# First matrix of each feed-forward as 2x2x2 block products: seven products in place of eight, sums of blocks formed on chip

## The chip, the cores and the metric

The kernel runs on one core of a Trainium2 chip. The metric is the device time of one launch in microseconds. Before the change it is 1934.65 us, the median of three runs (1934.33 to 1936.84).

The engines that matter: TensorE (PE in the profile; its weight loads are PEld) multiplies, VectorE (DVE) and ScalarE (ACT) work elementwise, SyncE (SP) only issues the transfers here, and GpSimd (POOL) sets a few tiles to zero.

## The reference

Two layers of three sublayers each: a feed-forward, a mixer (attention and a short convolution side by side) and a second feed-forward. The model width is 1024, there are 512 tokens, and a feed-forward has 2816 hidden columns, each with a gate and an up column. Everything is in single precision. The mixer's inside is not touched by the change.

```python
def _swiglu(h, w1, w2):
    g, up = jnp.split(h @ w1, 2, axis=-1)
    return (jax.nn.silu(g) * up) @ w2
...
def reference(x, c, w_ada, b_ada, norm_g, w_in, q_norm_g, k_norm_g, conv_w, conv_b,
              w_out, ffn_w1, ffn_w2):
    b = x.shape[0]
    for layer in range(DEPTH):
        mod = (jax.nn.silu(c) @ w_ada[layer] + b_ada[layer]).reshape(b, N_SUB, N_MOD, D_MODEL)
        shift = mod[:, :, 0, None, :]
        scale = mod[:, :, 1, None, :]
        gate = mod[:, :, 2, None, :]
        def ada(z, i):
            return _rmsnorm(z, norm_g[layer, i]) * (1.0 + scale[:, i]) + shift[:, i]
        x = x + 0.5 * gate[:, 0] * _swiglu(ada(x, 0), ffn_w1[layer, 0], ffn_w2[layer, 0])
        x = x + gate[:, 1] * _mixer(ada(x, 1), w_in[layer], q_norm_g[layer], k_norm_g[layer],
                                    conv_w[layer], conv_b[layer], w_out[layer])
        x = x + 0.5 * gate[:, 2] * _swiglu(ada(x, 2), ffn_w1[layer, 1], ffn_w2[layer, 1])
    return x
```

## The kernel before

All activations are kept transposed: channels on the partitions, the 512 tokens along the free axis, so x is eight tiles of 128x512. Every operand of the big products is held as two halves, a rounded one (hi) and the rest (lo), and a product of two operands is three matmuls: hi by hi, hi by lo, lo by hi (`product`, lines 173 to 177). The names in the trace are whi, wlo for weights, hh, hl for the normed input, hidh, hidl for the hidden tiles.

**Weights.** A unit is a block of 128x1024 (some 128x768) that is loaded into a raw tile by SP (four buffers); ScalarE copies it to whi (line 126) and VectorE subtracts to get wlo (line 127), with five buffers for each of the two. `weights` (line 143) hands out units in the fixed order of `_units` and lets `fetch` load and split two units ahead of the one in use.

**A feed-forward** (`ffn`, line 409) runs its 22 hidden tiles in three parts of 8, 8 and 6 (`PARTS`). For a hidden tile, a gate unit and an up unit are multiplied with the eight input tiles, each 8 x 3 matmuls of 512 columns into a PSUM bank (`gemm`); `finish` takes SiLU of the gate on ScalarE, multiplies by the up bank on VectorE (line 431) and splits the result (lines 319, 320). Behind a part, `Tail.run` (line 339) multiplies its hidden tiles with the second matrix, eight output tiles, and VectorE adds each into x (line 333). In the last part the last three output tiles are taken half by half of the tokens (256 columns), so that the next norm of the first half (sums of squares, `inv_rms`, `spread`, `modulate`) runs beside the products of the second half. `begin` (line 395) starts a feed-forward with four units of which first the one token half and then the other is multiplied, in the order in which `modulate` delivers tiles.

**Jobs.** The shift, scale and gate vectors of the next sublayers are dot products: a load of 512 KB and a VectorE operation of 128x1024 with a sum (`ada_job`, line 192). 16 of them stand in the start, the other 128 are queued by `later` and taken out by `next_job`: two behind each hidden tile, one behind each unit of the second matrix.

**Order.** The instructions are traced in program order; a list scheduler of the compiler then orders each engine's queue by that priority and by what is ready, and puts in the semaphores. Steps such as `inv_rms` are put among the products by counting product columns (`after`, `tick`).

## Time and profile before

| | before |
|---|---|
| median of three runs | 1934.65 us |
| span of the profiled execution | 1934.5 us |
| TensorE busy | 1909.2 us (99%), 9460 matmuls |
| VectorE busy | 1090.5 us (56%) |
| ScalarE busy | 675.0 us (35%) |
| moved by DMA | 253.95 MB, mean 131 GB/s |

The span reaches from the first to the last instruction of one execution. Busy time counts how long at least one instruction of the engine was running. Matmuls overlap, so the pitch between the starts of two of them says more than the duration of one. A line of the timeline gives the start, the duration, the engine, the line of the kernel, the operation and its tiles; "x3" is three instructions merged. In brackets stands the idle time before it and what ended it.

### The profile page before, as it was taken

The numbers are of one execution on the slowest core, as the hardware profiler recorded it, in microseconds if no ns is written. First come the engines' busy times: TensorE is split into PE (matmuls) and PEld (weight loads), VectorE is DVE, ScalarE is ACT, GpSimd is POOL, SyncE is SP. The second block draws the span as 40 slices with busy tenths as digits, with TensorE's granted clock in tenths as the row PEclk, the third lists the DMA queues.
The fourth block names the chain that finished last, engine by engine and source line by source line (L and its number), as shares of the span: only waits on it lengthen the run. The fifth ranks groups of instructions, "written<-read, shape, count | busy, mean of one in ns | idle before, by whom it ended". The sixth has DMA issues, their size and how long they took to land.

```text
span 1934.5 us, 24290 instructions
## 1 busy us (share of the span) xinstructions
PE 1909.2 (99%) x9460; PEld 1619.8 (84%) x9460; DVE 1090.5 (56%) x2074; ACT 675.0 (35%) x1110; POOL 12.2 (1%) x76
## 2 busy tenths in 40 slices
PE   6999999999999999999999999999999999999999
PEld 4888888899889888888898888888898898888888
DVE  8664564587866564433465545456977755333333
ACT  3322222355653322222332222223756533222121
POOL 0000000000000000000000000000000000000000
PEclk9999999999999999999999999999999999999999
DMA  8664564312223464222325646542222315222221
GB/s 340 207 218 156 170 218 131 109 55 68 97 66 121 147 219 157 99 98 90 122 98 190 211 149 197 184 130 77 78 76 88 109 66 177 96 98 98 98 82 60
DMA packets 73573, 253.95 MB, mean 131 GB/s; under 512 B 8049, under 2 KB 9073, under 8 KB 73458
## 3 DMA queue, kind: packets, MB, share of 16 engines
q1 hardware_dynamic: 73458, 252.40, 38.9%
q8 instruction: 74, 1.21, 0.3%
q14 instruction: 41, 0.34, 0.1%
HBM read 250.27 MB, written 2.10 MB: 130 GB/s over the span
## 4 chain that ended last, share of the span: by engine, by line
PE 98%; DVE 1%; DMA 0%; issue 0%; ACT 0%; SPq 0%; DVEq 0%
PE acc L175 31%; PE acc L177 30%; PE acc L176 30%; PE sb L530 1%; PE tp L521 1%; PE tp L550 1%; PE sb L175 1%; PE sb L176 1%; PE sb L177 1%; PE sb L560 1%; PE sb L561 1%; DVE ada L196 0%; DMA ada<-in_w_ada 0%; PE tp L290 0%; DVE ssq L282 0%; DVE wlo L127 0%
## 5 line engine op out<-in xcount | busy, mean ns | idle before, releaser
L126 ACT ACTIVATE whi<-raw 128x1024 fp32r<-128x1024 f32 (+1 forms) x344 | 350.0, 1021 | 986.7 <-PE acc L176 877.5
L175 PE MATMUL acc<-hh,whi 128*128 128x512 f32 (+1 forms) x1760 | 673.3, 384 | 0.0
L177 PE MATMUL acc<-hh,wlo 128*128 128x512 f32 (+1 forms) x1760 | 669.4, 381 | 0.0
L176 PE MATMUL acc<-hl,whi 128*128 128x512 f32 (+1 forms) x1760 | 665.5, 378 | 0.0
L127 DVE TENSOR_TENSOR wlo<-raw,whi 128x1024 fp32r<-128x1024 f32 (+1 forms) x344 | 402.8, 1174 | 245.9 <-ACT whi L126 217.5
L177 PEld LDWEIGHTS acc<-hh,wlo 128*128 128x128 f32 x1760 | 330.9, 188 | 66.1 <-DVE wlo L127 0.2
L176 PEld LDWEIGHTS acc<-hl,whi 128*128 128x128 f32 x1760 | 331.3, 188 | 62.3
L175 PEld LDWEIGHTS acc<-hh,whi 128*128 128x128 f32 x1760 | 331.1, 188 | 58.5 <-ACT whi L126 0.4
L175 PE MATMUL acc<-hidh,whi 128*128 128x512 f32 (+1 forms) x776 | 287.3, 370 | 0.0
L177 PE MATMUL acc<-hidh,wlo 128*128 128x512 f32 (+1 forms) x776 | 286.7, 369 | 0.0
L176 PE MATMUL acc<-hidl,whi 128*128 128x512 f32 (+1 forms) x776 | 286.6, 369 | 0.0
L333 DVE SCALAR_TENSOR_TENSOR x<-acc,fin,x 128x512 f32<-128x512 f32 (+1 forms) x130 | 87.9, 676 | 228.8 <-PE acc L177 228.3
L431 DVE TENSOR_TENSOR sg<-acc,sg 128x512 f32<-128x512 f32 x84 | 58.0, 691 | 252.4 <-PE acc L177 252.4
L196 DVE SCALAR_TENSOR_TENSOR ada<-ada,cb 128x1024 f32<-128x1024 f32 x144 | 172.2, 1221 | 17.5 <-DMA ada<-in_w_ada 11.2
L176 PEld LDWEIGHTS acc<-hidl,whi 128*128 128x128 f32 x776 | 146.3, 188 | 25.0
L177 PEld LDWEIGHTS acc<-hidh,wlo 128*128 128x128 f32 x776 | 146.2, 188 | 24.8
L175 PEld LDWEIGHTS acc<-hidh,whi 128*128 128x128 f32 x776 | 146.2, 188 | 24.8
L175 PE MATMUL acc<-whi,hh 128*128 128x384 f32 x256 | 89.5, 350 | 2.6 <-ACT hh L314 2.6
L176 PE MATMUL acc<-wlo,hh 128*128 128x384 f32 x256 | 86.6, 338 | 0.0
L177 PE MATMUL acc<-whi,hl 128*128 128x384 f32 x256 | 85.5, 339 | 0.0
L314 ACT ACTIVATE hh<-z,fin 128x256 fp32r<-128x256 f32 (+1 forms) x88 | 41.5, 522 | 58.0 <-DVE z L312 55.7
L320 DVE TENSOR_TENSOR hidl<-sg,hidh 128x512 fp32r<-128x512 f32 x88 | 60.0, 685 | 0.0
(89 smaller groups left out, 1308.3 us busy)
## 6 DMA issues: line engine op xcount, KB each, us to landing
raw<-in_w SPq DMA_DIRECT2D x176, 512.0 KB, 3.5
ada<-in_w_ada SPq DMA_DIRECT2D x128, 512.0 KB, 4.6
raw<-in_w2a SPq DMA_DIRECT2D x64, 512.0 KB, 3.5
raw<-in_w2b SPq DMA_DIRECT2D x32, 384.0 KB, 3.1
raw<-in_w_qkv SPq DMA_DIRECT2D x32, 384.0 KB, 3.1
raw<-in_w_gcu SPq DMA_DIRECT2D x24, 512.0 KB, 3.5
ada<-in_w_ada SPq DMA_DIRECT2D x8, 1024.0 KB, 8.4
raw<-in_w_out SPq DMA_DIRECT2D x16, 512.0 KB, 3.5
```

Of the source, the lines that this page charges most:

```text
L126: nc.scalar.activation(hi, raw, AF.Copy)
L127: nc.vector.tensor_tensor(out=lo, in0=raw, in1=hi.bitcast(F32), op=ALU.subtract)
L175: nc.tensor.matmul(out, a[0], b[0], start=first, stop=False)
L176: nc.tensor.matmul(out, a[0], b[1], start=False, stop=False)
L177: nc.tensor.matmul(out, a[1], b[0], start=False, stop=last)
L196: nc.vector.scalar_tensor_tensor(w, w, 1.0, cb, op0=ALU.mult, op1=ALU.mult, accum_out=raw[:, m, j:j + 1])
L314: nc.scalar.activation(hh[j][:, cols], z, AF.Identity, bias=shift)
L320: return nc.vector.tensor_tensor(out=lo, in0=v, in1=hi.bitcast(F32), op=ALU.subtract)
L333: nc.vector.scalar_tensor_tensor(x[j][:, cols], ps, gate, x[j][:, cols], op0=ALU.mult, op1=ALU.add)
L431: nc.vector.tensor_tensor(out=sg, in0=pu, in1=sg, op=ALU.mult)
L521: nc.tensor.transpose(pt[:, c * 128:(c + 1) * 128], p[:, c * 128:(c + 1) * 128], ident)
L530: nc.tensor.matmul(ps, v[c][:, i], z[:, c], start=c == m == 0, stop=c == n - 1 and m == 1)
```

## The change

The first matrix of a feed-forward is multiplied in blocks. The output of a pair of hidden tiles has two block rows (gate, up) and two block columns (first and second half of the tokens); the contraction has two blocks (the even and the odd tiles of the input). That would be eight block products. In Winograd's form of Strassen's algorithm there are seven:

| product | weights | tokens |
|---|---|---|
| 1 | gate, even | even, first half |
| 2 | gate, odd | odd, first half |
| 3 | gate odd - S | odd, second half |
| 4 | up, odd | V4 = odd first half - V6 |
| 5 | T = up even + up odd | V5 = even second half - even first half |
| 6 | S = T - gate even | V6 = odd second half - V5 |
| 7 | gate even - up even | V7 = odd second half - even second half |

One product is one unit of weights: two hidden tiles x four tiles of its contraction block x three, 24 matmuls of 256 columns. VectorE forms the four weight sums of each pair of hidden tiles in the raw tiles (`split_unit`), before the split in two halves, so a pair has seven units to split instead of four. Seven blocks are loaded for a pair instead of four (two gate blocks a second time). The four token sums are formed once for each norm, with the second token half (`Blocks.half`), and h becomes four tiles that hold seven operands each. Bank a of a pair takes products 1, 6, 7 and 4 one behind the other and is copied out by ScalarE in between (`done`), bank c takes 5 and 3, bank b takes 2; the other sums are VectorE's additions.

Around it: `_ffn_order` writes the order of units out by hand (products 1 and 2 of three pairs first, since they need the first token half alone; then the others of the first four pairs interleaved; from the fifth on pair by pair); the accumulation banks go from 4 and 2 to one group of 6; raw tiles go from 4 to 6 and now serve the jobs' loads too; weights are loaded two units further ahead than they are split; whi and wlo go from 5 to 4 and the separate buffers for the last units of the second matrix go; the last part begins with two output tiles side by side; the jobs of a third sublayer's gate move into the feed-forward before it; three jobs stand beside each of the first four pairs of the kernel, one beside each other pair, two behind each unit of the second matrix. In the mixer some small tiles move into the unused part of h.

```diff
-PARTS = ((0, 8), (8, 8), (16, 6))
-# The order of a mixer's products: q, k, v of pairs of heads, and the channel tiles of the convolution.
+NP = NF // 2
+PARTS = ((0, 4), (4, 4), (8, 3))
...
+LOADED = 2
...
+MOVING = {2: 0, 1: 1, 3: 2, 5: 3, 7: 4, 6: 5, 4: 6}
...
+def _ffn_order():
+    order = [[(0, 1), (0, 2)], [(1, 1), (1, 2)], [(2, 1)], [(2, 2)], [(0, 5), (0, 6)]]
+    order += [[u] for u in ((1, 5), (0, 7), (1, 6), (0, 4), (0, 3), (2, 5), (1, 7), (2, 6), (1, 4), (1, 3), (3, 1),
+                            (2, 7), (3, 5), (2, 4), (2, 3), (3, 6), (3, 2), (3, 7))]
+    ends = [p0 + n - 1 for p0, n in PARTS]
+    for n in range(3, NP):
+        if n > 3:
+            order += [[(n, 5)], [(n, 6)]]
+            if n - 1 in ends:
+                order += [[("part", ends.index(n - 1))]]
+            order += [[(n, 2)], [(n, 7)]]
+        if n + 1 < NP:
+            order += [[(n + 1, 1)]]
+        order += [[(n, 4)], [(n, 3)]]
+    return order + [[("part", len(PARTS) - 1)]]
...
-        return psum.tile([128, 512], F32, name="acc", tag="acc", bufs=4)
+        return psum.tile([128, 512], F32, name="acc", tag="acc", bufs=6)
...
+    s_bank = acc_bank
+    def half_kb(name):
+        return tmp.tile([128, S], F32, name=name, tag="ev", bufs=7)
...
+    def raw_tile(name="raw"):
+        return wp.tile([128, 1024], F32, name=name, tag="raw", bufs=6)
...
+        pool, bufs = place.get(key, (wp, 4))
...
+    def load_unit(key, src, n):
+        if key[0] != "w1":
+            return [load(src, n)]
+        b11, b12, b21, b22 = (src[b] for b in range(4))
+        return [load(b) for b in {1: (b11,), 2: (b12,), 3: (b12,), 4: (b22,), 5: (b21, b22), 6: (b11,), 7: ()}[key[4]]]
+    def split_unit(key, raws, n):
+        if key[0] == "w1":
+            pair, which = key[:4], key[4]
+            def combine(out, a, b, op):
+                nc.vector.tensor_tensor(out=out, in0=a, in1=b, op=op)
+            if which == 5:
+                a21, s = raws
+                combine(s, a21, s, ALU.add)
+                blocks[pair] = [a21, s]
+                raws = [s]
+            elif which == 6:
+                (a11,), (a21, s) = raws, blocks[pair]
+                combine(s, s, a11, ALU.subtract)
+                blocks[pair].append(a11)
+                raws = [s]
+            elif which == 7:
+                a21, _, a11 = blocks[pair]
+                combine(a11, a11, a21, ALU.subtract)
+                raws = [a11]
+            elif which == 3:
+                (a12,), s = raws, blocks.pop(pair)[1]
+                combine(a12, a12, s, ALU.subtract)
+        return halves(key, raws[0], n)
...
+        for i in range(len(loaded), min(upto + LOADED, len(order))):
+            loaded.append(load_unit(*order[i]))
         for i in range(len(fetched), min(upto, len(order))):
-            fetched[i] = split_weights(*order[i])
+            key, _, n = order[i]
+            fetched.append(split_unit(key, loaded[i], n))
+            loaded[i] = None
...
+    def shared_bulk(out, a, b, first):
+        for i, (p, q) in enumerate(((a[0], b[0]), (a[0], b[1]), (a[1], b[0]))):
+            nc.tensor.matmul(out, p, q, start=first and i == 0, stop=i == 2, skip_group_check=True)
+        tick(out.shape[-1])
...
+            w = ada_load(raw_tile("ada"), l, s, m, j)
...
+            if l == 0:
+                gate(0, 0)
             norm(l, 1)
             gate(l, 1)
             norm(l, 2)
+            gate(l, 2)
         elif l + 1 < DEPTH:
             norm(l + 1, 0)
-    # ---- norms ----
+            gate(l + 1, 0)
...
+        return [base.tile([128, 7 * S], F32R, name="h", tag="h", bufs=KD // 2) for _ in range(KD // 2)]
...
+    def moving(h, k, which):
+        o = MOVING[which] * 512
+        return h[k][:, o:o + 256], h[k][:, o + 256:o + 512]
+    def scaled(z, l, s, rb, cols, j):
+        nc.vector.scalar_tensor_tensor(z, x[j][:, cols], mods[l, s][1][:, 1, j:j + 1], rb, op0=ALU.mult, op1=ALU.mult)
+    def shifted(hi, lo, l, s, z, j):
+        shift = mods[l, s][1][:, 0, j:j + 1]
+        nc.scalar.activation(hi, z, AF.Identity, bias=shift)
+        nc.vector.scalar_tensor_tensor(lo, z, shift, hi.bitcast(F32), op0=ALU.add, op1=ALU.subtract)
+    def modulate(h, l, s, rb, cols, j):
+        hh, hl = plain(h)
+        z = half_kb("z")[:, :cols.stop - cols.start]
+        scaled(z, l, s, rb, cols, j)
+        shifted(hh[j][:, cols], hl[j][:, cols], l, s, z, j)
+    class Blocks:
+        def __init__(self, l, s, h, pool):
+            self.l, self.s, self.h, self.pool = l, s, h, pool
+            self.first = [pool.tile([128, KD, 256], F32, name="hva", tag="hva", bufs=1)]
+        def half(self, rb, which, k):
+            l, s, h, cols = self.l, self.s, self.h, HALVES[which]
+            first = self.first[0]
+            a, b = 2 * k, 2 * k + 1
+            if which == 0:
+                for j, product in ((a, 1), (b, 2)):
+                    scaled(first[:, j], l, s, rb, cols, j)
+                    shifted(*moving(h, k, product), l, s, first[:, j], j)
+                return
+            z = half_kb("z").rearrange("p (i n) -> p i n", i=2)
+            v = self.pool.tile([128, 4, 256], F32, name="hvb", tag="hvb", bufs=2)
+            scaled(z[:, 0], l, s, rb, cols, a)
+            scaled(z[:, 1], l, s, rb, cols, b)
+            shift = mods[l, s][1][:, 0, b:b + 1]
+            nc.vector.tensor_tensor(out=v[:, 0], in0=z[:, 0], in1=first[:, a], op=ALU.subtract)
+            nc.vector.scalar_tensor_tensor(v[:, 2], z[:, 1], shift, v[:, 0], op0=ALU.add, op1=ALU.subtract)
+            shifted(*moving(h, k, 3), l, s, z[:, 1], b)
+            nc.vector.scalar_tensor_tensor(v[:, 1], z[:, 1], steps_of[l, s][:, k:k + 1], z[:, 0],
+                                           op0=ALU.add, op1=ALU.subtract)
+            nc.vector.scalar_tensor_tensor(v[:, 3], first[:, b], shift, v[:, 2], op0=ALU.add, op1=ALU.subtract)
+            o = MOVING[5] * 512
+            to = h[k][:, o:o + 2048].rearrange("p (c i n) -> p c i n", i=2, n=256)
+            split(to[:, :, 0], to[:, :, 1], v)
...
+            if side_by_side:
+                banks = [acc_bank() for _ in range(2)]
+                for j in range(2):
+                    ws[j] = weights(*key, j)
+                    products(banks[j], j, slice(0, S), range(n - side_by_side))
+                for j in range(2):
+                    products(banks[j], j, slice(0, S), range(n - side_by_side, n))
+                    self.add(j, banks[j], slice(0, S), done)
+                next_job(4)
+                j0 = 2
...
+            fetch(used[0] + 4 - SPLIT)
...
+    def evacuation(l, which, hid_pool):
+        banks, sums_of = {}, {}
+        hid = {}
+        def silu(v):
+            nc.scalar.activation(v, v, AF.Silu)
+        def added(n, i, bank):
+            v = sums_of[n, i]
+            nc.vector.tensor_tensor(out=v, in0=bank, in1=v, op=ALU.add)
+            return v
+        def copied(n, i):
+            sums_of[n, i] = half_kb("ev")
+            nc.scalar.activation(sums_of[n, i], banks[n, "a"], AF.Copy)
+        def hidden(n, half, gate, up):
+            if n not in hid:
+                hp = hid_pool[0]
+                hid[n] = [hp.tile([128, 2, S], F32R, name=m, tag=m, bufs=PARTS[0][1]) for m in ("hidh", "hidl")]
+            v = half_kb("hid")
+            nc.vector.tensor_tensor(out=v, in0=up, in1=gate, op=ALU.mult)
+            a, b = [z[:, :, HALVES[half]] for z in hid[n]]
+            ended[:] = [split(a, b, v.rearrange("p (f n) -> p f n", f=2))]
+        def done(n, p):
+            if p == 1:
+                copied(n, 1)
+            elif p == 2:
+                silu(added(n, 1, banks.pop((n, "b"))))
+            elif p == 6:
+                copied(n, 2)
+            elif p == 7:
+                copied(n, 3)
+                added(n, 3, banks[n, "c"])
+            elif p == 4:
+                hidden(n, 0, sums_of.pop((n, 1)), banks.pop((n, "a")))
+            elif p == 3:
+                gate = added(n, 2, banks.pop((n, "c")))
+                silu(gate)
+                hidden(n, 1, gate, sums_of.pop((n, 3)))
+                sums_of.pop((n, 2))
+        return banks, done, hid
+    BANKS = {1: "a", 6: "a", 7: "a", 4: "a", 2: "b", 5: "c", 3: "c"}
+    def feed(l, which, h, group, banks, done):
+        opened = set()
+        ws = []
+        for n, p in group:
+            ws.append(weights("w1", l, which, n, p))
+            if p in (1, 2, 5):
+                banks[n, BANKS[p]] = acc_bank()
+                opened.add((n, p))
+        for k in range(KD // 2):
+            for (n, p), w in zip(group, ws):
+                for f in range(2):
+                    o = (f * 4 + k) * 128
+                    shared_bulk(banks[n, BANKS[p]][:, f * 256:f * 256 + 256], [v[:, o:o + 128] for v in w],
+                                moving(h, k, p), (n, p) in opened and k == f == 0)
+        for n, p in group:
+            done(n, p)
+    def ffn(l, s, h, carried, groups=()):
         which = s // 2
         tail = Tail(l, s)
         later(l, s)
+        pool = []
+        banks, done, hid = evacuation(l, which, pool)
+        todo = _ffn_order()
+        if groups:
+            todo = todo[groups[1]:]
+            groups[0](banks, done)
+        while todo[0][0][1] in (1, 2):
+            feed(l, which, h, todo.pop(0), banks, done)
+        flush()
+        carried.close()
+        stack = ExitStack()
+        pool.append(stack.enter_context(tc.tile_pool(name="hid", bufs=1)))
+        for group in todo:
+            if group[0][0] != "part":
+                feed(l, which, h, group, banks, done)
+                if s == l == 0 and group[0][0] < PARTS[0][1]:
+                    next_job(group[0][1] in (7, 4, 3))
+                else:
+                    next_job(group[0][1] == 3)
+                continue
+            p = group[0][1]
+            p0, np = PARTS[p]
+            ks = [[z[:, f] for z in hid[n]] for n in range(p0, p0 + np) for f in range(2)]
+            room = None
+            if p == len(PARTS) - 1 and s == 2 and l + 1 < DEPTH:
+                room = stack.enter_context(tc.tile_pool(name="next", bufs=1))
+            out = tail.run(ks, ("w2", l, which, p), p == len(PARTS) - 1, room, 2 if p == len(PARTS) - 1 else 0)
+        next_job(len(jobs))
+        return out, stack
...
+    def side_by_side(banks, done):
+        groups = _ffn_order()[:2]
+        feed(0, 0, h, groups[0] + groups[1], banks, done)
+    groups = (side_by_side, 2)
...
+    w1 = a["ffn_w1"].reshape(DEPTH, 2, KD // 2, 2, 128, 2, NP, 2, 128)
+    out["w1"] = c(w1.transpose(0, 1, 6, 5, 3, 4, 7, 2, 8).reshape(DEPTH, 2, NP, 4, 128, D))
```

## Rows read from the trace of the kernel before

**Rows 1.** The page: busy time by engine, and the chain that ended last.
```profile
PE 1909.2 (99%) x9460; PEld 1619.8 (84%) x9460; DVE 1090.5 (56%) x2074; ACT 675.0 (35%) x1110; POOL 12.2 (1%) x76
...
PE 98%; DVE 1%; DMA 0%; issue 0%; ACT 0%; SPq 0%; DVEq 0%
```

**Rows 2.** Busy time by stretch (length, engines, PEclk, DMA, GB/s): first feed-forward, first mixer.
```profile
23.80:393.70 369.90, 367.52 (x1644) 303.01 (x1644) 216.19 (x320) 106.02 (x134) 0.34 (x3) 1.00 0.53 182
...
393.70:610.00 216.30, 215.29 (x1229) 191.69 (x1230) 164.60 (x470) 123.46 (x277) 5.47 (x35) 1.00 0.26 83
```

**Rows 3.** Timeline of TensorE (start, us, engine, line, operation), full products, first and last.
```profile
100.28 0.39 PE L175 MATMUL acc<-hh,whi 128*128 128x512 f32 x1
...
111.95 0.39 PE L175 MATMUL acc<-hh,whi 128*128 128x512 f32 x1
```

**Rows 4.** Timeline of TensorE, first and last of three runs of half-wide products.
```profile
598.85 0.28 PE L175 MATMUL acc<-hh,whi 128*128 128x256 f32 x1
...
609.33 0.28 PE L177 MATMUL acc<-hh,wlo 128*128 128x256 f32 x1
...
967.09 0.28 PE L175 MATMUL acc<-hidh,whi 128*128 128x256 f32 x1
...
975.61 0.28 PE L177 MATMUL acc<-hidh,wlo 128*128 128x256 f32 x1
...
990.09 0.28 PE L176 MATMUL acc<-hl,whi 128*128 128x256 f32 x1
...
1004.14 0.28 PE L177 MATMUL acc<-hh,wlo 128*128 128x256 f32 x1
```

**Rows 5.** Timeline of VectorE, operations that follow each other without a gap.
```profile
29.46 1.22 DVE L196 SCALAR_TENSOR_TENSOR ada<-ada,cb 128x1024 f32<-128x1024 f32 x1
...
30.61 1.22 DVE L127 TENSOR_TENSOR wlo<-raw,whi 128x1024 fp32r<-128x1024 f32 x1
31.75 0.15 DVE L202 TENSOR_TENSOR fin<-mod,par 128x2 f32<-128x2 f32 x1
...
982.50 1.26 DVE L312 SCALAR_TENSOR_TENSOR z<-x,fin,tp 128x256 f32<-128x256 f32 x3
983.67 1.27 DVE L315 SCALAR_TENSOR_TENSOR hl<-z,fin,hh 128x256 fp32r<-128x256 f32 x3
...
1005.56 0.68 DVE L431 TENSOR_TENSOR sg<-sb,sg 128x512 f32<-128x512 f32 x1
1006.16 0.68 DVE L431 TENSOR_TENSOR sg<-acc,sg 128x512 f32<-128x512 f32 x1
```

**Rows 6.** VectorE around two norms: the start as a stretch (columns as rows 2), then timeline.
```profile
20.94:54.85 33.91, 30.20 (x112) 23.14 (x113) 33.77 (x62) 10.54 (x13) 0.00 (x0) 0.95 0.71 270
...
987.22 0.15 DVE L260 TENSOR_SCALAR sm<-tp 128x2 f32<-128x2 f32 x1
...
988.99 0.16 DVE L265 SCALAR_TENSOR_TENSOR sm<-sm 128x2 f32<-128x2 f32 x1
```

**Rows 7.** TensorE behind a wait in the start: timeline, then the stretch (columns as rows 2).
```profile
42.81 0.63 PE L176 MATMUL sb<-hl,whi 128*128 128x512 f32 x1
43.24 0.63 PE L177 MATMUL sb<-hh,wlo 128*128 128x512 f32 x1
...
40.80:60.00 19.20, 19.13 (x77) 15.52 (x78) 14.74 (x32) 5.27 (x8) 0.00 (x0) 0.91 0.42 151
```

**Rows 8.** Transfers: the first stretch (columns as rows 2), and the weight loads of the page.
```profile
0.00:40.80 40.80, 21.83 (x70) 14.76 (x70) 31.39 (x63) 16.31 (x21) 0.20 (x4) 1.00 0.91 347
...
raw<-in_w SPq DMA_DIRECT2D x176, 512.0 KB, 3.5
```

**Rows 9.** ScalarE's copies (timeline), and who waited for them (us in total, times, longest).
```profile
1005.24 2.00 ACT L126 ACTIVATE whi<-raw 128x1024 fp32r<-128x1024 f32 x2
1007.14 1.15 ACT L319 ACTIVATE hidh<-sg 128x512 fp32r<-128x512 f32 x2
...
DVE wlo L127 <- ACT whi L126: 217.5, 121, 9.0
```

More of the change, by code (lines that the diff above doesn't have):

```diff
@@ L1 @@
 import math
[L2 removed]
+from contextlib import ExitStack, nullcontext
 import numpy as np
@@ new lines, in mixer, with load_ada @@
+        stack = ExitStack()
+        op = stack.enter_context(tc.tile_pool(name="out", bufs=1))
+        for j in range(KD - SPLIT, KD):
+            place["out", l, j] = op, SPLIT
+        return tail.run(ks, ("out", l), True, op), stack
+    mod_tile(0, 0)
+    stack = ExitStack()
+    sp = stack.enter_context(tc.tile_pool(name="start", bufs=1))
+    ada = []
+    def load_ada():
+        ada.append(sp.tile([128, 2, D], F32, name="ada", tag="ada", bufs=3))
+        nc.sync.dma_start(ada[-1], t["w_ada"][0, 0:2 * KD].rearrange("(m j) p n -> j p m n", m=2)[len(ada) - 1])
@@ new lines, in trunk @@
+    c = sp.tile([1, D], F32, name="c")
+    nc.sync.dma_start(c, t["c"])
+    load_ada()
+    load_ada()
+    for j in range(KD):
+        nc.sync.dma_start(x[j], t["xT"][j])
+    nc.sync.dma_start(par, t["par"])
+    nc.sync.dma_start(ident, t["ident"])
+    for half in range(2):
+        ps = acc_bank()
+        cols = slice(half * 512, half * 512 + 512)
+        nc.tensor.matmul(ps, row, c[:, cols], start=True, stop=True)
+        nc.scalar.activation(cb[:, cols], ps, AF.Silu)
+    acc = sums()
```

223 lines of the change are left out of this document (81 added, 142 removed).

## The prediction

> **What bounds the kernel now.** I read the engine summary and the chain of work that ended last first, then the busy time by stage, then single instructions. TensorE is busy for 99% of the 1934.5 us, and 98% of the chain that ended last is TensorE; VectorE stands at 56% [rows 1]. The stages say the same without the average: a feed-forward is TensorE from end to end, and VectorE has the most work in the first one (216 of 370 us) [rows 2]. So time is gained only by taking columns of products away, and it is lost wherever another engine is made later than TensorE. A full product of 512 columns is issued every 0.2288 us (51 of them from 100.28 to 111.95) [rows 3]. Durations of one matmul overlap the next, so I go by pitches.
>
> **Part 1, what goes.** The first matrix takes 44 units x 8 tiles x 3 = 1056 full products in a feed-forward, 4224 in all; in the last three feed-forwards 96 of them are already run as 192 half-wide ones. After the change it is 11 pairs x 7 products x 8 x 3 = 1848 matmuls of 256 columns each, 7392 in all, so the price of a half-wide matmul decides. The trace has it in three stretches: 89 from 598.85 to 609.33 (0.1178 us), 124 from 990.09 to 1004.14 (0.1133) and 71 from 967.09 to 975.61 (0.1200) [rows 4]. I take 0.1178, the middle one, which has the same kind of operand (normed input), and keep the other two as bounds. Before: (1056 + 2880) x 0.2288 + 576 x 0.1178 = 968.4 us. After: 7392 x 0.1178 = 870.8. **TensorE gains 97.6 us** (128 at 0.1133, 83 at 0.1200). One eighth would be 121; the rest goes because two halves cost 0.2356 and one whole 0.2288.
>
> The Trainium skill, "TensorE: Matmul & The Clock Gate" (Back-to-back issue gap), speaks against this: it gives sustained pitches of about 81 ns at 128 columns and 131 ns at 512, by which a line puts a half-wide product at three quarters of a whole one. With that ratio the 7392 would take 7392 x 0.171 = 1264 us and the kernel would come out near 2230 us. Rows 4 show about half instead, so this stays a rival with one chance in a hundred.
>
> **Part 2, what VectorE gets.** Back to back, a 1024-wide two-input operation takes 1.14 us, a modulation job 1.15, a 512-wide one 0.60 and a 256-wide one 0.39 to 0.40 [rows 5]. A pair of hidden tiles (two gate, two up) now needs four block sums and seven subtractions for the low halves, 11 x 1.14 = 12.5 us, and seven operations of 512 after the products, 4.2 us: **16.7 us a pair**. Before it was 4 x 1.14 + 4 x 0.60 = 7.0. TensorE needs 7 x 24 x 0.1178 = 19.8 us for the pair. With the one modulation job that stands beside most pairs VectorE stands at 17.9 of 19.8 us; with the three of the first four pairs of the kernel at 20.2. In the steady part TensorE still ends last, but VectorE has no reserve to catch up with. Products 1 and 2 are the cheap ones for it and they stand first, so the backlog after a norm lasts for about four pairs.
>
> **Part 3, the three later feed-forwards.** From the instant at which the first half of a norm is ready, VectorE owes: 16 operations of 0.40 for the first token half (6.4, as before), the last sums of squares and additions (1.5), the second root (1.9) [rows 6], the second half with its token sums, 4 x (6 x 0.40 + 0.35 + 1.14) = 15.6 (before: 16 x 0.40 = 6.4), four pairs (67.0) and the low half of the next product 1 (1.1), less what can be split ahead (2.3) and the last evacuations, which nobody waits for (3.6), plus three jobs (3.5; none in the last feed-forward). That is 91 us; 92 in the third, where one weight buffer comes free late, 88 in the last. At 96% use (an estimate; in the start, where it has work waiting from 20.94 to 54.85 us, it is busy for 33.77 of 33.91 us, but there it seldom waits for ScalarE [rows 6]), and with the last unit's 2.8 us of products behind it, TensorE is through these 29 units after 97.7, 98.9 and 94.1 us. Its own work is 1.1 + 29 x 2.83 = 83.2. **Lost: 14.5 + 15.7 + 10.9 = 41 us** (30 if VectorE is never idle, 60 at 90%).
>
> **Part 4, the start.** From the first root (20.94 us [rows 6]) VectorE owes 12 jobs (13.8), the blocks (22.0), twelve small ones (1.8), four pairs (67.0), one more low half (1.1) and 11 jobs (12.7), less 3.6: 114.8 us, 119.6 at 96%. TensorE is through 29 units at 143.3 us; 48 units (135.8) and the second matrix (474 x 0.2288 + 108 x 0.1200 = 121.4) follow, to 400.5 us. Before, the mixer began at 393.7 [rows 2]. So the first feed-forward is 6.8 us longer, where its products alone would have made it 23.9 shorter: **lost 30.7 us** (26 if VectorE is never idle, 39 at 90%).
>
> **Part 5, the rest.** (a) The split weights have 4 buffers instead of 5 and the last three units of the second matrix lie among them, so the next stage begins with one unit split ahead instead of up to four; in the mixer, a head pair holds all four. I take 6 us for both mixers and the entries to them (0 to 15). (b) TensorE that waits is granted a lower clock: in the start, behind a wait for the norm, full products come every 0.43 us, which is the lower of the two levels (1.2 GHz), against 0.2288 at the upper one, and the granted clock of that stretch is 0.91 [rows 7]. I take 3 us for the three stalls (0 to 8). (c) Seven loads of 512 KB a pair instead of four are 185 GB/s, 265 in the first four pairs; the start moves 347, and a load lands in 3.5 us while it is issued four units (11.3 us) ahead [rows 8]. Nothing, unless a job's tile blocks the queue: jobs now share the six raw buffers, and a weight load queued behind a job's load on SP waits with it. (d) ScalarE gets three more copies of 0.95 us and the evacuation copies, 10.3 of 19.8 us a pair [rows 9]: beside other work. (e) The bank that products 1, 6, 7 and 4 share has to be copied out between them; one unit (2.8 us) of other products stands in each gap, and a copy of 512 takes about 0.5 us [rows 9]: nothing. (f) The eight jobs of a third sublayer's gate move into the feed-forward before it (first 56 jobs instead of 48, last none instead of 8), 9.2 us of VectorE and eight loads on SP; two go beside each unit of the second matrix, where VectorE has 8 x (1.14 + 0.60 + 2.30) = 32 of 43.9 us: nothing, and if that cover were gone, 9 us.
>
> Sum: 1934.5 - 97.6 + 41.1 + 30.7 + 9 = **1918 us**. The span is the profiled execution's own time; the median of the runs is 1934.65.
>
> **The rivals.** *Faster, 1887 us:* the half-wide products run at 0.1133 as in one of the three stretches; that takes 31 us more. With a VectorE that is never idle behind the norms (16 more) it is 1871. For it: that run is the second token half of a feed-forward's first units, the nearest thing to the new products. Against it: the other run with normed input is at 0.1178, and nothing in the trace says what sets the three levels. *Slower, 1960 us:* VectorE's queue is in order, and a block sum has to go to ScalarE for its high half (0.95 us and the handover) before VectorE can subtract. Already now VectorE spends 217.5 us in 121 such waits [rows 9]. Four chains a pair are 4.4 us if nothing fills them; from 3.1 us of idle time a pair (1.9 with a job) VectorE ends later than TensorE everywhere. Half uncovered: 16 pairs behind the norms x 2.2 = 35, and 28 others x 0.25 = 7, so 42 more; wholly uncovered, 70 + 69, which is 2057. Against it: the compiler that orders these queues has kept TensorE at 99% through the mixer, where VectorE is at 76% with many small steps [rows 2]. The same page of the Trainium skill (its table of the engine) calls VectorE's and ScalarE's queues strict FIFO with 8 entries, which would let this happen; it changes no price. *No gain, 1932 to 1946:* a pitch of 0.1200 (14 us less gained), with part 5 as taken or at its upper bounds.
>
> **How the numbers follow.** Forecast 0.45 (its own range 1900 to 1938), faster rival 0.24, slower 0.27, no gain 0.03, the skill's ratio 0.01. The range 1876 to 1962 reaches to the faster rival with some of its extra, and to the slower at half its price; outside lie the wholly uncovered waits (about 0.12) and the lowest corner (0.06). A measurement of this kernel tells about 0.2%, 4 us, from no change. Faster by more than that: 0.40 of the forecast and the faster rival, 0.64. Same: 0.05 and half of the no-gain case and what of the slower one falls there, 0.10. Slower: 0.26.
>
> **What would show it.** Right: steady pairs of about 19.8 us with TensorE without gaps, VectorE above 85% there, and TensorE waiting for low halves or token blocks of VectorE in the 100 us behind each norm, 10 to 16 us in all; a first mixer that begins near 400 us, where it began at 393.7. Wrong: pairs of 21 us and more with VectorE waiting for ScalarE (slower rival); waits shorter than 8 us behind the norms (the backlog was hidden); TensorE waiting for loads, or for banks.

## The result, and the profile after

The changed kernel takes **1958.9 us** (median of 4; 1956.4 to 1964.7), beside 1934.9 for the kernel before on the same chip: 1.0127 times as long, 95% interval 1.0110 to 1.0144. It is slower by 1.3% where 1918 us and "faster" were forecast. The profiled execution has a span of 1958.9 us; before it was 1934.5, so 24.4 us came on top.

The page of the changed kernel: busy time by engine, the chain that ended last by engine and by line, and the groups of the weight sums and the modulation jobs (busy, mean ns, idle before them and who ended it).

```profile
PE 1856.1 (95%) x12340; PEld 1718.4 (88%) x12340; DVE 1551.4 (79%) x2593; ACT 898.7 (46%) x1382; POOL 11.9 (1%) x76
...
PE 67%; DVE 17%; DMA 10%; issue 3%; ACT 3%; DVEq 0%; ACTq 0%
PE acc L258 31%; PE acc L251 11%; PE acc L252 10%; PE acc L253 10%; DMA ada<-in_w_ada 8%; DVE wlo L164 4%; DVE ada L282 4%; DVE raw L185 2%; ACT whi L163 2%; DMA raw<-in_w 2%; PE acc L739 1%; DVE h L458 1%; DVE ev L559 1%; PE tp L730 1%; PE tp L759 1%
...
L185 DVE TENSOR_TENSOR raw<-raw 128x1024 f32<-128x1024 f32 x176 | 214.5, 1221 | 33.6 <-DMA raw<-in_w 32.2
L282 DVE SCALAR_TENSOR_TENSOR ada<-ada,cb 128x1024 f32<-128x1024 f32 x144 | 175.3, 1223 | 59.8 <-DMA ada<-in_w_ada 53.4
```

Beside the kernel before [rows 1] TensorE is busy for 53 us less and is no longer the whole chain (67% for 98%). VectorE holds 17% of it, and **transfers hold 10%, most of them loads of modulation jobs**, which no term of my sum had.

The products of the first matrix (L258) fall into three stretches a feed-forward, with the parts of the second matrix between them. Busy time by stretch (length, then PE, PEld, DVE, ACT, POOL, PEclk, DMA share, GB/s): the first two stretches of each of the four feed-forwards.

```profile
23.16:151.01 127.85, 103.42 (x745) 99.26 (x745) 120.60 (x180) 56.75 (x75) 0.00 (x0) 0.95 0.61 209
194.54:280.26 85.72, 82.05 (x674) 81.84 (x672) 76.19 (x85) 44.48 (x55) 0.00 (x0) 0.96 0.62 209
...
644.18:746.19 102.01, 92.07 (x753) 90.99 (x752) 95.71 (x135) 56.08 (x75) 0.00 (x0) 0.95 0.46 151
789.72:873.82 84.10, 81.30 (x673) 81.09 (x672) 75.52 (x83) 44.56 (x55) 0.00 (x0) 0.98 0.61 208
...
1007.50:1112.07 104.57, 94.09 (x747) 92.56 (x747) 95.59 (x136) 54.30 (x73) 0.00 (x0) 0.94 0.44 147
1155.62:1242.45 86.83, 82.33 (x673) 82.12 (x672) 75.81 (x85) 44.45 (x55) 0.00 (x0) 0.96 0.63 207
1603.51:1704.04 100.53, 91.46 (x752) 90.79 (x751) 94.20 (x131) 57.12 (x75) 0.00 (x0) 0.95 0.45 147
1747.58:1827.09 79.51, 79.51 (x673) 79.51 (x672) 67.11 (x71) 44.36 (x55) 0.00 (x0) 1.00 0.53 173
```

The last line is the steady state: 28 units (four pairs, 672 matmuls) in 79.51 us, TensorE without a gap, 0.1183 us a matmul, 19.9 us a pair, VectorE at 84%. By that pitch the first stretches (744 matmuls of products; the counts in the lines hold a few others) would be 88.0 us and the middle ones 79.5. What they are longer is what each place loses: 39.8 in the start, 14.0, 16.6 and 12.5 behind the three norms; 6.2, 4.6, 7.3 and 0 behind the first parts; 4.2, 0, 1.6 and 0 behind the second parts. In the last feed-forward, which has no jobs, nothing is lost behind a part.

Three kinds of wait that the kernel before does not have, one of each, in the timeline of TensorE (start, us, engine, line, operation, idle before it and its releaser): behind a norm, behind a part, and at the end of the first mixer.

```profile
659.05 0.39 PE L258 MATMUL acc<-h,whi 128*128 128x256 f32 x2
667.88 0.77 PE L258 MATMUL acc<-h,whi 128*128 128x256 f32 x2 [8.44 <-DVE ev L559]
...
670.58 0.63 PE L258 MATMUL acc<-h,whi 128*128 128x256 f32 x2
671.22 0.63 PE L258 MATMUL acc<-h,whi 128*128 128x256 f32 x2
...
206.89 0.80 PE L258 MATMUL acc<-h,whi 128*128 128x256 f32 x2 [3.67 <-ACT ev L564]
...
590.45 0.82 PE L730 MATMUL tp<-ident,p 128*128 128x128 f32 x6
593.60 1.43 PE L730 MATMUL tp<-ident,p 128*128 128x128 f32 x8 [2.34 <-DVE pl L458]
```

Behind the 8.44 us wait two matmuls and the third that stands with them take 0.64 us (670.58 to 671.22), 0.213 each. The granted clock of these microseconds is 0.50, the lower level (1.2 GHz), where the steady state has 0.1183 at 1.00 (2.4 GHz). The same view as above, from the wait on:

```profile
667.88:671.65 3.77, 3.50 (x15) 3.20 (x16) 3.77 (x5) 2.89 (x4) 0.00 (x0) 0.50 0.43 138
```

### The profile page after: what moved, and what is told of

It reads as the page before. It is cut to its first block, busy times and chain, and to the rows that moved or that the text cites. A ratio compares the mean times of both kernels' runs of the same rounds, so it can differ in the third digit from the quotient of the medians.

```text
span 1958.9 us, 31198 instructions
## 1 busy us (share of the span) xinstructions
PE 1856.1 (95%) x12340; PEld 1718.4 (88%) x12340; DVE 1551.4 (79%) x2593; ACT 898.7 (46%) x1382; POOL 11.9 (1%) x76
## 4 chain that ended last, share of the span: by engine, by line
PE 67%; DVE 17%; DMA 10%; issue 3%; ACT 3%; DVEq 0%; ACTq 0%
PE acc L258 31%; PE acc L251 11%; PE acc L252 10%; PE acc L253 10%; DMA ada<-in_w_ada 8%; DVE wlo L164 4%; DVE ada L282 4%; DVE raw L185 2%; ACT whi L163 2%; DMA raw<-in_w 2%; PE acc L739 1%; DVE h L458 1%; DVE ev L559 1%; PE tp L730 1%; PE tp L759 1%
## 5 line engine op out<-in xcount | busy, mean ns | idle before, releaser
L258 PE MATMUL acc<-h,whi 128*128 128x256 f32 x4928 | 905.6, 287 | 59.7 <-DVE ev L559 25.5
L258 PEld LDWEIGHTS acc<-h,whi 128*128 128x128 f32 x4928 | 776.8, 193 | 67.6 <-issue 26.0
L163 ACT ACTIVATE whi<-raw 128x1024 fp32r<-128x1024 f32 (+1 forms) x476 | 487.2, 1032 | 649.5 <-PE acc L252 298.0
L258 PE MATMUL acc<-h,wlo 128*128 128x256 f32 x2464 | 703.0, 286 | 11.4 <-DVE wlo L164 11.2
L164 DVE TENSOR_TENSOR wlo<-raw,whi 128x1024 fp32r<-128x1024 f32 (+1 forms) x476 | 562.4, 1187 | 90.1 <-ACT whi L163 85.2
L258 PEld LDWEIGHTS acc<-h,wlo 128*128 128x128 f32 x2464 | 475.3, 193 | 14.7 <-DVE wlo L164 14.5
L185 DVE TENSOR_TENSOR raw<-raw 128x1024 f32<-128x1024 f32 x176 | 214.5, 1221 | 33.6 <-DMA raw<-in_w 32.2
L251 PE MATMUL acc<-h,whi 128*128 128x512 f32 (+1 forms) x368 | 139.8, 380 | 0.0
L252 PE MATMUL acc<-h,whi 128*128 128x512 f32 (+1 forms) x368 | 134.9, 367 | 0.0
L253 PE MATMUL acc<-h,wlo 128*128 128x512 f32 (+1 forms) x368 | 134.7, 366 | 0.0
L559 DVE TENSOR_TENSOR ev<-acc,ev 128x512 f32<-128x512 f32 x132 | 90.5, 687 | 9.5 <-PE acc L258 9.5
```

The costliest lines, as they stand in the source:

```text
L163: nc.scalar.activation(hi, raw, AF.Copy)
L164: nc.vector.tensor_tensor(out=lo, in0=raw, in1=hi.bitcast(F32), op=ALU.subtract)
L185: nc.vector.tensor_tensor(out=out, in0=a, in1=b, op=op)
L251: nc.tensor.matmul(out, a[0], b[0], start=first, stop=False)
L252: nc.tensor.matmul(out, a[0], b[1], start=False, stop=False)
L253: nc.tensor.matmul(out, a[1], b[0], start=False, stop=last)
```

## The experiments

All are edits of the changed kernel. Times are medians; each was run beside the kernel before, which stood at 1934.8 to 1935.7 us.

**The weight sums on GpSimd (e1).** Theory: VectorE's load is the limit.

```
-                nc.vector.tensor_tensor(out=out, in0=a, in1=b, op=op)
+                nc.gpsimd.tensor_tensor(out=out, in0=a, in1=b, op=op)
```

> The four block sums of the weights of each pair of hidden tiles run on GpSimd instead of VectorE, nothing else moves. Theory (VectorE's backlog behind the norms and in the start costs what the stages show: 12 to 17 us in the first stretch of each later feed-forward and some 33 in the first): VectorE loses 4 x 1.14 us a pair, 18 us in the first four pairs, so the first stretches come down by 6 to 12 us in the three later feed-forwards and by about 15 in the first, and the kernel to 1910 to 1930 us. The stalls behind the parts of the second matrix stay. Rival (what holds TensorE there is the chain load, sum, copy, subtraction and its latency, not VectorE's sum of work): a sum on another engine makes that chain longer, the first stretches stay within 3 us or grow, and the kernel stays at 1955 us or above.

2059.5 us, ratio 1.064 (1.062 to 1.066). From the groups of e1: the sums on GpSimd, and VectorE's 1024-wide low halves beside them.

```profile
L185 POOL TENSOR_TENSOR raw<-raw 128x1024 f32<-128x1024 f32 x176 | 471.1, 2679 | 1087.3 <-DMA raw<-in_w 571.4 <-DVE wlo L164 156.4 <-DVE ada L282 153.5
L164 DVE TENSOR_TENSOR wlo<-raw,whi 128x1024 fp32r<-128x1024 f32 x412 | 629.3, 1532 | 207.5 <-ACT whi L163 203.7
```

A sum takes 2679 ns there and 1221 on VectorE, and VectorE's own work becomes slower beside it: these low halves take 1532 ns in the mean for 1222 (the 768-wide ones of the mixers, where GpSimd forms no sums, 954 for 957). The run says nothing about VectorE's load, because it lengthened the way of four of a pair's seven weights.

**The jobs without their loads (e2).**

```
-            w = ada_load(raw_tile("ada"), l, s, m, j)
+            nc.vector.scalar_tensor_tensor(raw_tile("ada"), cb, 1.0, cb, op0=ALU.mult, op1=ALU.mult,
+                                           accum_out=raw[:, m, j:j + 1])
+            return
```

> The 128 queued modulation jobs keep their VectorE operation and their turn of a raw tile, but multiply the constant vector with itself, and their 512 KB loads are left out (the modulation is not the reference's). Theory (behind the parts of the second matrix TensorE waits because the jobs' loads and the weight loads share six raw tiles, three of which a pair holds across the part): the stretches of the first matrix behind the parts, 85.7, 84.1 and 86.8 us in the first three feed-forwards, come down to the 79.5 of the last one, which has no jobs, and the last stretches of 56.9 and 54.3 to 52.7; the kernel to about 1935 us. Rival (the jobs' VectorE time of 1.15 us each is what delays): these stretches stay within 1 us of what they are and the kernel stays above 1950.

1943.8 us, 15 less, where about 1935 was expected. The middle stretches of the first three feed-forwards come to 81.2 us each, for 85.7, 84.1 and 86.8; two of those behind the norms grow (103.9 and 107.4 us for 102.0 and 104.6). The first of the middle ones, as above:

```profile
193.72:274.96 81.24, 80.53 (x676) 80.02 (x674) 68.94 (x76) 42.60 (x54) 0.00 (x0) 1.00 0.47 152
```

VectorE did the same work (1550 us for 1551), so it is the jobs' loads that cost time behind the parts. Whether they take tiles or bandwidth, this run can't tell: it frees both.

**No weight sums (e3).**

```
-                nc.vector.tensor_tensor(out=out, in0=a, in1=b, op=op)
+                pass
```

> The four block sums of the weights are left out altogether (products 5, 6, 7 and 3 take single blocks, so the result is not the reference's); loads, splits, products and evacuations stay. It bounds what moving the sums can bring: theory (VectorE's backlog) 1905 to 1925 us, with the first stretches of the later feed-forwards at 90 to 96 us instead of 100.5 to 104.6; what is left there is the token blocks of the second half, 16 us of VectorE in one piece. Rival (latency of the chain): about 1.2 us less on each unit's way and hardly any change of the stretches, 1950 or more.

1915.7 us. The start's first stretch is 12.0 us shorter (115.85), but those behind the norms only 2.2, 2.7 and 0.7 (99.82, 101.90, 99.81), though VectorE is busy for 16.5 to 18.5 us less in each. Behind the norms, then, its sum of work over four pairs isn't the first limit. The first stretch of the second feed-forward, and the middle one of the first, as above:

```profile
619.98:719.80 99.82, 91.67 (x752) 91.00 (x751) 78.79 (x119) 56.47 (x75) 0.00 (x0) 0.95 0.48 159
...
182.29:261.81 79.52, 79.52 (x673) 79.52 (x672) 55.89 (x63) 43.32 (x55) 0.00 (x0) 1.00 0.61 209
```

The largest part of the 43 us that e3 gains lies behind the parts: all stretches there are at the steady pitch (79.5 and 45.4 us), 23.9 us in all, with every load in place. That doesn't make VectorE's work the limit there: without the sums, two of the three raw tiles of the next paragraph aren't held across a part either, so the run changes two things at once.

**The part one pair-step later (e4).** Products 5 and 6 of the next pair stand ahead of each part and hold three of the six raw tiles until the weight sums of 7 and 3, which stand behind it. Here the part waits until 2 and 7 are done too, so one tile is held.

```
             if n > 3:
                 order += [[(n, 5)], [(n, 6)]]
-                if n - 1 in ends:
-                    order += [[("part", ends.index(n - 1))]]
                 order += [[(n, 2)], [(n, 7)]]
+                if n - 1 in ends:
+                    order += [[("part", ends.index(n - 1))]]
```

> The first and second part of the second matrix stand two units later, behind products 5, 6, 2 and 7 of the next pair instead of behind 5 and 6, so that only one raw tile of that pair (its sum) is held across the part instead of three. Theory (raw tiles held across the part starve the loads of jobs and weights): the stretches of the first matrix behind the parts lose most of their 5 to 7 us, 12 to 20 us in all, and the kernel comes to 1939 to 1947 us. Rival (the rate of the transfers, 264 to 290 GB/s beside the parts, is the limit, or the jobs' place on the queue): the stretches stay and the kernel stays within 4 us of 1959.

1939.7 us (10 runs), ratio 1.0020 (1.0011 to 1.0030). The middle stretches of e4, of the first three feed-forwards (columns as above):

```profile
200.89:280.40 79.51, 79.51 (x673) 79.51 (x672) 71.54 (x79) 44.64 (x55) 0.00 (x0) 1.00 0.63 211
...
786.39:866.31 79.92, 79.79 (x673) 79.58 (x672) 74.39 (x85) 44.27 (x55) 0.00 (x0) 1.00 0.68 222
...
1147.33:1227.12 79.79, 79.79 (x674) 79.63 (x673) 73.61 (x84) 43.86 (x55) 0.00 (x0) 1.00 0.67 222
```

All three are within half a microsecond of the steady state, with every job and load in place, and 19 of the 24 us are gone. The rate of the transfers wasn't the limit: e4 moves more beside the first part than the changed kernel does, and loses nothing behind it (the part, changed kernel and then e4, columns as above).

```profile
151.01:194.54 43.53, 43.53 (x194) 36.04 (x193) 33.43 (x48) 10.39 (x12) 0.00 (x0) 1.00 0.87 290
157.79:200.89 43.10, 43.10 (x193) 35.68 (x192) 36.07 (x52) 9.41 (x10) 0.00 (x0) 1.00 0.88 312
```

How the tiles cost time stands in the chain of the changed kernel from the part to the wait of 3.67 us (start, us, what):

```profile
171.54 4.20 DMA ada<-in_w_ada
...
175.83 1.25 DVE ada L282 x2
177.08 0.02 issue
177.10 4.38 DMA ada<-in_w_ada
...
181.57 1.25 DVE ada L282 x2
...
197.03 4.63 DMA raw<-in_w
...
201.78 0.06 DVE raw L185
...
204.06 0.69 DVE ev L559
...
206.36 0.49 ACT ev L564
...
206.89 3.14 PE acc L258 x13
```

A job's tile comes free, the next load starts at once, lands some 4.4 us later, is worked off, and so on: 5.6 us for each turn with two jobs (171.54 to 177.10), while a unit of the second matrix takes 5.4 (43.5 us for eight). Counted from the loads and the last reader of each tile, all six raw tiles are taken throughout: each of the 34 loads into them between 140 and 210 us starts within 0.08 us of another tile's release. Of the three tiles in question one goes at 154.6 already, because VectorE makes the sum of product 7 early; the others stay until 190 and 199, which is nearly the whole part. So the loads of the next weights come late, and what waits for them holds up others: the one at 197.03 is for a product 5, its sum (201.78) stands in VectorE's queue ahead of an addition (204.06), and that addition ahead of the copy on ScalarE (206.36) that empties the bank for the product at 206.89.

**The token blocks of the second half in two steps (e5, e8, e9; on e4).** First what products 5 and 6 multiply, then what 3, 7 and 4 do: in e5 the second step comes 2048 columns after the first (SECOND), in e8 at the flush ahead of the first product 5, behind the split of the weights of 5 and 6; e9 is e8 without the weight sums.

```
-            split(to[:, :, 0], to[:, :, 1], v)
+                split(to[:, 0:4:2, 0], to[:, 0:4:2, 1], v)
+                return
...
+            split(to[:, 1:4:2, 0], to[:, 1:4:2, 1], z)
...
                 after(0, lambda: change(1, r[1]))
+                if blocks:
+                    after(SECOND, lambda: change(2, r[1]))
```

> Beside the later part of e4: the token blocks of the second half are made in two steps, first what products 5 and 6 multiply (8.8 us of VectorE by rows of before: 16 operations of 0.40 and four of 0.60), then what 7, 4 and 3 multiply (7.2 us); 16.0 us instead of 15.6, so VectorE has slightly more to do over the first four pairs. Theory (the stall behind a norm is the time that the blocks of the second half take in one piece, against the six units that can go ahead of them): the 8.4 to 8.6 us waits behind the three norms shrink to under 3 us, the first stretches of the last three feed-forwards go from 102.0, 104.6 and 100.5 us to 91 to 95, the first one loses 0 to 8, and the time is 1900 to 1915 us. Rival (my prediction's: VectorE's sum of work over four pairs): stretches and time stay, 1938 to 1943.

1943.4 us, ratio 1.0043.

> As e5, but the second step of the token blocks (what products 7, 4 and 3 multiply, 7.2 us of VectorE) is put behind the weights of the first products 5 and 6 in VectorE's queue; in e5 it stood ahead of them, and TensorE waited 4.6 to 6.0 us for the low half of product 6's weights. Theory (a latency: what VectorE has to do between the second root and the seventh unit): of e5's waits of 2.1 and 4.6 us behind each of the three norms under 3 us are left together, first stretches with the two units before the part 99 to 103 us instead of 107.7, 109.5 and 106.2 in e4, and the time 1918 to 1930. Rival (VectorE's sum of work over four pairs): the wait appears again some units later, stretches 105 to 108, time 1936 to 1943.

1949.7 us, ratio 1.0082.

> e8 without the four weight sums of each pair (left out of the computation), 4.6 to 4.9 us less of VectorE in every pair. With the sums left out alone (e3) the stretches behind the norms lost only 0.7 to 2.7 us. If a latency and VectorE's sum of work are two limits of nearly the same height, one behind the other, this run frees both: first stretches of 95 to 99 us (the products alone need 93.7 for 33 units), time 1895 to 1910. If only the latency counts, the same as e8, less 12 us in the first feed-forward. If neither, e4's 106 to 109.

1911.2 us. First stretches of the second feed-forward of e4, e5, e8 and e9 (792 matmuls of products, 93.7 us by the steady pitch):

```profile
635.18:742.86 107.68, 97.89 (x801) 96.80 (x800) 101.05 (x142) 59.32 (x79) 0.00 (x0) 0.95 0.48 157
```
```profile
634.43:742.89 108.46, 99.87 (x800) 98.29 (x799) 101.95 (x146) 60.77 (x83) 0.00 (x0) 0.95 0.49 158
```
```profile
635.89:745.49 109.60, 100.33 (x801) 98.41 (x799) 101.83 (x146) 60.95 (x83) 0.00 (x0) 0.95 0.48 157
```
```profile
621.75:723.84 102.09, 97.20 (x801) 96.20 (x799) 84.18 (x130) 59.84 (x83) 0.00 (x0) 0.98 0.52 170
```

My theory of a latency fell. The one wait of 8.4 us became two, and moved: in e5 2.10 for the last block and 4.56 for the low half of product 6, in e8 2.10, then 3.72 and 1.34 for the high halves of summed weights, some five units later:

```profile
667.80 0.80 PE L259 MATMUL acc<-h,whi 128*128 128x256 f32 x2 [3.72 <-ACT whi L164]
```

Only e9 shortens the stretch, and by more (7.5 us less than e8) than the sums gave alone (2.2): as soon as the order lets TensorE go on, VectorE's sum of work ends last, and as soon as there is less work, the order does. By these runs both limits are there and nearly as high. They aren't the whole: e9's stretch is still 8.4 us above the pitch, 4.9 of them without a matmul, and these I have not taken apart.

**The last values in another tile (e6; on e4).**

```
-        turns = {"v": 0, "abb": 0}
+        turns = {"v": 6, "abb": 0}
```

> Beside the later part of e4: the attention values of the last head group go to the second h tile instead of the first. Theory (the output products of a mixer begin late because their high and low halves go to the h tiles whose spare part still holds the last values of the attention): with the first tile free the first output products fill the gaps of the last attention steps, the 2.3 us wait at the end of each mixer goes, mixer and outputs together take 224 to 226 us instead of 228.3, and the time is 1932 to 1937. Rival (the split weights' four buffers, as in my part 5a): no change, 228 us and 1938 to 1942.

1937.9 us; mixers with outputs 228.2 and 228.0 us for 228.4 and 228.3, the waits 2.05 and 2.04 for 2.32. My theory of the spare part fell.

**Two jobs instead of three in the start (e10; on e8 and e6).** 

> e8 with the last head group's values in the second h tile (as in e6) and two modulation jobs instead of three beside the first three pairs of the kernel (three jobs fewer, 3.5 us of VectorE, done at the feed-forward's end). Expected 2 to 5 us less in the first feed-forward than e8 by VectorE's sum of work, 0 to 0.5 in the mixers; 0 to 2 if the loads of the start are what it waits for.

1950.7 us, no change; the start with its first 33 units is 0.4 us longer than in e8 (136.7 for 136.4). Three jobs less gave nothing where 18 us of sums gave 12 (e3). This stays unexplained.

**The banks apart (e11; on e4).** The kernel before had four accumulator banks and two for the attention; the change made one group of six.

```
-        return psum.tile([128, 512], F32, name="acc", tag="acc", bufs=6)
+        return psum.tile([128, 512], F32, name="acc", tag="acc", bufs=4)
-    s_bank = acc_bank
+    def s_bank():
+        return psum.tile([128, 512], F32, name="sb", tag="sb", bufs=2)
-                banks[n, BANKS[p]] = acc_bank()
+                banks[n, BANKS[p]] = acc_bank() if p == 1 or (n, p) == (2, 2) else s_bank()
```

> Beside the later part of e4: the accumulator banks are two groups again, as in the kernel before: four for the products of weights with normed tokens and two for the attention's scores and weighted values (in a feed-forward the two serve products 2 and 5, but for the second pair behind the first two, whose product 2 takes one of the four). Theory (in the mixer, scores, weighted values and the convolution's products share six banks, and the last attention steps hold those that the first output products need): the output products stand among the last attention steps again, the 2.3 us wait at each mixer's end goes, mixer and outputs take 223 to 225 us instead of 228.3, and the time is 1928 to 1936. Rival (the split weights' four buffers in place of five, my part 5a): mixers stay at 228, 1938 to 1942. In the feed-forwards nothing should change; if a bank comes free late there, the stretches grow by 1 to 3 us each.

**1932.0 us** (11 runs), ratio 0.9981 (0.9972 to 0.9990): a little faster than the kernel before. Mixer with outputs, and the 22 us at the end of its attention, in e4 and then in e11:

```profile
406.80:635.18 228.38, 224.54 (x1282) 199.94 (x1282) 170.94 (x489) 124.81 (x280) 5.16 (x31) 0.99 0.25 82
...
570.00:592.00 22.00, 19.57 (x99) 16.01 (x98) 17.83 (x40) 13.40 (x28) 0.69 (x4) 0.92 0.14 48
```
```profile
405.93:630.14 224.21, 222.78 (x1282) 198.84 (x1282) 170.94 (x489) 124.42 (x280) 5.08 (x31) 0.99 0.25 83
1349.90:1572.49 222.59, 221.18 (x1283) 197.31 (x1282) 171.04 (x489) 124.44 (x280) 5.13 (x31) 1.00 0.25 84
573.00:595.00 22.00, 22.00 (x116) 18.14 (x115) 20.06 (x38) 16.19 (x31) 0.69 (x4) 1.00 0.14 48
```

With the banks apart output products stand among the last attention steps again, and in these 22 us TensorE has no gap and a granted clock of 1.00 (0.92 in e4). The mixers take 224.2 and 222.6 us, where the kernel before has 222.8 and 222.6 (its first one, as above; the second from 1345.75 to 1568.33):

```profile
393.70:616.47 222.77, 221.76 (x1284) 198.16 (x1285) 169.60 (x489) 125.18 (x281) 5.47 (x35) 1.00 0.25 81
```

**The evacuation ahead of the blocks (e12; on e11).**

```
-                after(0, lambda: change(1, r[1]))
+                after(256, lambda: change(1, r[1]))
```

> e11 with one order changed: the evacuation of the first pair's product 2 (and the low half of product 5's weights) stands ahead of the second half's token blocks in VectorE's queue, not behind them; in e11 the wait of 8.4 to 8.6 us behind each norm ends with that evacuation. If TensorE waits there for the bank: the wait shrinks by 3 us or more, and it then waits for the last token block, whose place moves back by 1.7 us at most, first stretches 104 to 106 us instead of 107.7, 110.6 and 106.5, time 1922 to 1930. If it waits for the token blocks themselves, or for VectorE's sum of work: stretches unchanged within 1 us, 1929 to 1934.

1931.0 us (6 runs), ratio 0.9971 (0.9959 to 0.9983), not to be told from e11; first stretches 107.8, 111.9 and 106.1. The wait stays and has another name, in the timeline of e12:

```profile
658.38 0.58 PE L259 MATMUL sb<-h,wlo 128*128 128x256 f32 x1 [8.37 <-DVE wlo L165]
```

So behind the norms no bank was short. Whatever stands behind the token blocks in VectorE's queue is named as the releaser: the evacuation, or the low half behind it.

## Why the prediction was wrong

The sum, term by term (us, against the span before):

| term | forecast | measured | more than forecast |
|---|---|---|---|
| products of the first matrix | -97.6 | -93.8 | 3.8 |
| start | 30.7 | 32.7 | 2.0 |
| three norms | 41.1 | 43.1 | 2.0 |
| mixers, entries, clock (measured: mixers 11.4, tails 8.5) | 9 | 19.9 | 10.9 |
| behind the parts | 0 | 23.9 | 23.9 |
| sum | -16.8 | 25.8 | 42.6 |

Measured: 7392 x 0.11832 = 874.6 for 968.4; the excess of the stretches above; for the start the later beginning of the mixer (415.78, so 22.1) plus the gain of the first feed-forward's products, 23.0 (1056 x 0.2288 less 1848 x 0.1183), less the 6.2 and 4.2 behind the parts and 2.0 in the tail, which is the time from the third stretch to the next sublayer. Mixers: 228.4 and 228.3 for 222.8 and 222.6, 11.4, and tails 2.0, 4.3, 1.8 and 0.4 longer than before. The clock has no term of its own here; it lies in the stretches. The spans differ by 24.4, so 1.4 us of the sum stay unexplained.

**The step that failed is 5c and 5f**, the jobs' loads at nothing. I compared rates (185 GB/s asked, 347 shown in the start) and looked at VectorE beside the second matrix. Neither ran out: e4 has the same jobs, moves 312 GB/s beside the first part and loses almost nothing behind it. What ran out was raw tiles: of six, three were held at the beginning of that part and two for nearly all of it, so a load could start only when a job or a unit gave its tile back. I had written the condition, "unless a job's tile blocks the queue", and that jobs share six tiles, and "TensorE waiting for loads, or for banks" stood among the signs of being wrong; but I had not counted who holds the tiles over the part. e2 (loads left out) shows that the loads matter, e4 (another order, all loads) that the held tiles do; e4 gives back 19 us. A seventh tile, which would show it by itself, was not tried.

**Part 5a** was the second: 6 us for the mixers and their entries by four split buffers. The mixers cost 11.4, and e11 shows that banks are the cause, which I had weighed in 5e for the feed-forward alone. In e11, which still has four split buffers, the mixers are at 224.2 and 222.6, so what I priced costs 1.4 and 0 in them. 5b, the clock: 3 us for three stalls; behind the 8.44 us 14 matmuls take 3.77 us (667.88 to 671.65; 0.28 of it is another wait) where the steady state would take 1.66, and there are ten waits above 2 us after the start, not three. Of the tails' 8.5 us, 3.8 are two waits for the norm ahead of the third feed-forward (2.41 and 1.40 us), where the kernel before waits 0.41; the rest I have not taken apart.

**Part 3** was right in size (43.1 for 41.1), and half right in mechanism. TensorE does wait in the 100 us behind each norm, but in one piece, after six units: VectorE has then been at the token blocks for 14 us without a gap (652.63 to 667.04), and everything that TensorE needs next stands behind them. e3 shows that the sum over four pairs isn't that limit; e5, e8 and e9 that it lies close behind it, and takes over as soon as the order is mended. **Part 4** held within 2 us; e3 (12 of 18 us) speaks for its sum of work and e10 against it.

**Part 1**: the middle pitch was right to 0.4% (0.1183 for 0.1178). The two sustained pitches of the Trainium skill ("TensorE: Matmul & The Clock Gate", Back-to-back issue gap), by which, on a line between them, a half-wide product would cost three quarters of a whole one, aren't borne out: 0.1183 beside 0.2288 is 0.52 [rows 3, 4].

**The rivals.** The slower one gave 1960 us and the time is 1959, but it was not this mechanism: steady pairs take 19.9 us without a gap and not 21 and more, so VectorE's waits for ScalarE are covered there. The faster one asked for a pitch of 0.1133, which didn't come. That the time agrees with the slower rival's price, and so lies in the range, is luck. What I lacked was a rival of buffers: I had listed only engines and pitches.

With e4's order and e11's banks the kernel is at 1932 us, 0.2% under the one before. The start and the norms take back 76 of the 94 us that the products give in the changed kernel, and in e11 the waits behind the norms are as long as there (8.43, 8.59 and 8.43 us).

## What to carry to other kernels

Before a load is costed at nothing, count the tiles of its pool over time, and who holds one across the longest stage; a free queue and free bandwidth don't help a load whose tile isn't free. When two uses are merged into one group of buffers or banks, go to every stage that draws from it, also those that the change doesn't name. The releaser of a long wait is only the instruction that happened to stand last: move it and see whether the wait stays before it is called the cause.

## What the runs showed of the hardware that was not expected

GpSimd took 2679 ns for a 1024-wide sum that VectorE does in 1221, and VectorE's operations on two tiles in SBUF became slower beside it: in the mean the 1024-wide low halves went from 1222 to 1532 ns and a 512-wide product of two tiles in SBUF from 687 to 928, while the same with one operand in the accumulator banks stayed at 681 (685 in the changed kernel).

```profile
L572 DVE TENSOR_TENSOR hid<-ev 128x512 f32<-128x512 f32 x44 | 40.8, 928 | 0.0
L572 DVE TENSOR_TENSOR hid<-acc,ev 128x512 f32<-128x512 f32 x44 | 30.0, 681 | 14.1 <-PE acc L258 14.1
```

The mean of 928 mixes two cases. In e1, 37 of these 44 products have no sum of GpSimd beside them and take 680 ns; the seven that have one beside them for over four fifths of their time take 2241. With one operand in the banks, ten have a sum beside them and take 685. Of the low halves, 275 have none beside them and take 1218.
